# A trunk of split-precision projections: high weights taken over 576 columns as 320 and 256 instead of 288 twice

## The chip, the core and the metric

The kernel runs on one core of one Trainium2 chip. The metric is device time in microseconds for one execution. An execution ends when the last of the twelve outputs is in device memory. Five engines work side by side, each in the order of its own instructions, and wait for each other by semaphores: TensorE (PE in the profile, PEld for its weight loads), VectorE (DVE), ScalarE (ACT), GpSimd (POOL) and SyncE (SP), which here only issues DMAs.

## The reference, cut to what matters

The program is one inference step of a two-layer streaming encoder for two groups of requests with the same weights: 256 new frames of one stream ("prompt") and 32 next frames of another ("sample"). Everything is float32.

```
# layer 0: retention heads beside gated linear attention heads; layer 1: band attention
def trunk(x, ...):
    for l in range(2):
        h = rmsnorm(x, p['norm_mix_g'][l])
        mix = ab_mixer(h, ...) if l == 0 else c_mixer(h, ...)
        x = x + mix
        h = rmsnorm(x, p['norm_ffn_g'][l])
        f, buf = conv_ffn(h, ...)
        x = x + f
    return rmsnorm(x, p['norm_final_g']), ...

def conv_ffn(h, conv_buf, w_up, conv_w, conv_b, w_down):
    up = jnp.einsum('btd,df->btf', h, w_up)            # 2048 -> 2 x 5632
    g, u = jnp.split(up, 2, axis=-1)
    gp = jnp.concatenate([hist, g], axis=1)
    gc = conv_b
    for w in range(3):
        gc = gc + gp[:, w:w + T] * conv_w[w]
    act = jax.nn.silu(gc) * u
    return jnp.einsum('btf,fd->btd', act, w_down), ...  # 5632 -> 2048
```

Nearly all the arithmetic is in the projections: `w_in` (2048 to 7184), `w_out` twice (2048 to 2048), `w_qkv` (2048 to 6144), and for each layer `w_ffn_up` and `w_ffn_down`.

## The kernel before

Activations stand transposed: features on the 128 partitions, the 288 tokens (256 of the prompt, 32 of the sample, `T`) along the free dimension. A projection to 128 output features is one "product". It runs over its input features in k-tiles of 128 and accumulates in one PSUM bank, tile `acc`, of which there are four.

To keep more of float32's digits than the fast fp32r format holds, each operand is split in a high part, rounded to fp32r, and a low part, the rest. For each k-tile `passes` (L80 to L85) issues three fp32r matmuls of 288 columns: high weights on high activations (L83), high weights on low activations (L84), low weights on high activations (L85). In what follows these three are a triple. Two activation stores feed them: `x` tiles (normalized inputs, one tile for each k-tile, high part and low part side by side) and `b` tiles (mixer outputs and gated FFN activations, likewise).

`weights` (L54) loads a chunk of up to eight k-tiles of weights, 512 KB, by a DMA on SP's queue; ACT rounds it into `wh` (L61) and DVE subtracts to get `wl` (L62). There are four buffers of `w` and three each of `wh` and `wl`. `project` (L65) strings chunks together to a product, `input_product` calls it for the `x` tiles. Behind a product, DVE reads the sum out of PSUM: in `ffn` it scales it (L307, L308, L322) or adds it to the residual (L332), in `out_proj` it adds it to the residual (L284).

`first_products` (L87) starts the kernel: it brings input and first weights in ten DMAs whose borders are `cuts`, and computes three sums side by side, two ordinary products (L121, L123, L125) and one narrow one of two matmuls for each k-tile (L126, L127). Eight small matmuls of ones (L95) stand ahead of it.

The residual `x` is too large to stay in SBUF during the first mixer, so it is loaded a second time from `xT` ahead of the first `out_proj`: four DMAs of four k-tiles each (L220), on SP's queue and so in a row with the weights. `out_proj` finishes three products whose first half was computed earlier (`started`), adds each to `x`, and prepares the next norm (`norm_in`, and `norm_stat` at L193, whose matmul by ones sums the squares at the end of a layer's half).

The order of instructions on each engine is that of a scheduler that interleaves the program's lines by their dependences, so products of one head run while vector work of another is done.

Of the kernel before, what the change touches and what calls it, by code (L numbers as in the profile page):

```python
# [17 lines left out]
T = TP + TS  # L18
FF = 5632
NF = FF // P  # L20
HALF = NF // 2
# [5 lines left out]
N_FIRST = 2  # L27
WCH = 8
# [9 lines left out]
class Trunk:  # L38
# [15 lines left out]
    def weights(self, src, n, lo=False):  # L54
# [6 lines left out]
        nc.scalar.copy(h, w)  # L61
        nc.vector.tensor_tensor(l, w, h.bitcast(F32), op=ALU.subtract)  # L62
        return h, l

    def project(self, src, xh, xl, nk, k0=0, chunks=None, part=None, ps=None):  # L65

        if ps is None:
            ps = self.acc_ps.tile([P, 512], F32, name="acc", tag="acc")[:, :T]
        chunks = chunks or range(0, nk, WCH)
        for c in chunks if part is None else chunks[part : part + 1]:  # L70
            n = min(WCH, nk - c)
            h, l = self.weights(src[:, k0 + c : k0 + c + n, :], n)
            for j in range(n):
                first, last = c == chunks[0] and j == 0, c == chunks[-1] and j == n - 1
                self.passes(ps, h[:, j, :], l[:, j, :], xh[c + j], xl[c + j], first, last)
        return ps

    def input_product(self, w):
        return self.project(w, self.xh, self.xl, KD)

    def passes(self, ps, h, l, xh, xl, first, last):
        nc = self.nc
        nc.tensor.matmul(ps, lhsT=h, rhs=xh, start=first, stop=False)  # L83
        nc.tensor.matmul(ps, lhsT=h, rhs=xl, start=False, stop=False)  # L84
        nc.tensor.matmul(ps, lhsT=l, rhs=xh, start=False, stop=last)  # L85

    def first_products(self, src, xw, lo_h):  # L87


        nc = self.nc  # L90
        ps = [self.acc_ps.tile([P, 512], F32, name="acc", tag="acc")[:, :T] for _ in range(N_FIRST + 1)]
        cuts = (0, 1, 2, 3, 4, 6, 8, 10, 12, 14, 16)
# [3 lines left out]
        for c, (i, j) in enumerate(zip(cuts, cuts[1:])):  # L96
# [9 lines left out]
            for k in range(i, j):  # L106
# [13 lines left out]
                for o in range(N_FIRST):  # L120
                    nc.tensor.matmul(ps[o], lhsT=h[:, at, o, :], rhs=self.xh[k], start=first, stop=False)  # L121
                for o in range(N_FIRST):
                    nc.tensor.matmul(ps[o], lhsT=h[:, at, o, :], rhs=self.xl[k], start=False, stop=False)  # L123
                for o in range(N_FIRST):
                    nc.tensor.matmul(ps[o], lhsT=l[:, at, o, :], rhs=self.xh[k], start=False, stop=last)  # L125
                nc.tensor.matmul(ps[-1], lhsT=lo[:, at, :], rhs=self.xh[k], start=first, stop=False)  # L126
                nc.tensor.matmul(ps[-1], lhsT=lo[:, at, :], rhs=self.xl[k], start=False, stop=last)  # L127
        return ps
# [67 lines left out]
    def run(self, ctx):  # L196
# [4 lines left out]
        xs = [self.const(f"x{k}", [P, 2, T], F32R) for k in range(KD)]  # L201
        self.xh, self.xl = [[x[:, i, :] for x in xs] for i in range(2)]
        b_all = self.const("b", [P, KD, 2, T], F32R)
        self.bh_all, self.bl_all = b_all[:, :, 0, :], b_all[:, :, 1, :]
        self.bh, self.bl = [[b_all[:, k, i, :] for k in range(KD)] for i in range(2)]
# [9 lines left out]
        with self.tc.tile_pool(name="x", bufs=1) as xp:  # L215
# [3 lines left out]
            for k in range(0, KD, 4):  # L219
                nc.sync.dma_start(x[:, k : k + 4, :], a["xT"][:, k : k + 4, :])  # L220
            self.out_proj(a["w_out_ab"], 1, (WCH, 0))
# [24 lines left out]
    def out_start(self, w, chunks, n):  # L246

        self.started = [self.project(w[m], self.bh, self.bl, KD, chunks=chunks, part=0) for m in range(n)]

    def start(self, pool):  # L250
# [21 lines left out]
        v1 = self.mm()[:, :T]  # L272
        second = lambda part: self.project(w[VB + 1], self.xh, self.xl, KD, chunks=(0, WCH), part=part, ps=v1)
# [3 lines left out]
    def out_proj(self, w, n, chunks):  # L277

        for m in range(KD):
            if m < len(self.started):  # L280
                ps = self.project(w[m], self.bh, self.bl, KD, chunks=chunks, part=1, ps=self.started[m])
            else:
                ps = self.project(w[m], self.bh, self.bl, KD, chunks=chunks)
            self.nc.vector.tensor_tensor(self.x[m], self.x[m], ps, op=ALU.add)  # L284
            self.norm_in(m, n)
        self.norm_stat()

    def ffn(self, pool, layer, n, x_all):
        nc, a = self.nc, self.a
        bs = [self._one(pool, f"b{k}", [P, 2, T], None, F32R) for k in range(KD, HALF)]  # L290
        bh, bl = [old + [b[:, i, :] for b in bs] for i, old in ((0, self.bh), (1, self.bl))]
# [8 lines left out]
        for half in range(2):  # L300
            for fl in range(HALF):
# [23 lines left out]
                self.split(bh[fl], bl[fl], v)  # L325
# [4 lines left out]
            for m in range(KD):  # L330
                ps = self.project(down[m], bh, bl, HALF, half * HALF)
# [753 lines left out]
```

## Time and profile before

| | us |
|---|---|
| time, median of 3 runs | 2677.67 (2677.26 to 2677.90) |
| time of the profiled execution | 2679.3 |
| span of the profiled execution | 2677.2 |
| PE busy | 2661.0 |
| DVE busy | 1560.8 |
| ACT busy | 1126.1 |
| mean DMA rate | 167 GB/s |

The profile page gives for each group of instructions the line, engine, operation and tiles, the shape written, the count, then the total busy time and the mean duration of one, then the idle time of the engine just ahead of the group with what ended it. The timeline gives start, duration, engine, line and tiles of single instructions; a PE row's duration reaches to a modelled end, and matmuls overlap, so that the distance between two starts tells more than a duration. The view of stretches gives the length, then for each engine its busy time and, in brackets, how many instructions it ran, then the granted clock, the share of DMA time and GB/s.

### The profile page before, as it was taken

What the parts mean: (1) busy time and instruction counts of PE and PEld (TensorE: products, weight loads), DVE (VectorE), ACT (ScalarE), POOL (GpSimd) and SP (SyncE); (2) the same over time, 40 slices, a digit from 0 to 9 for tenths busy, and PEclk for the clock granted to TensorE, in tenths of its full rate; (3) what the DMA queues carried; (4) which work ended last, traced back from release to release, by engine and by line L of the source; (5) the groups of instructions that cost most, each with busy time, mean ns of one, the idle gap of its engine ahead of it and who ended that gap; (6) DMA issues with size and microseconds to landing.
All of it is one profiled execution on the core that took longest, in us unless ns stands there. A gap on an engine that the chain in (4) does not pass through costs nothing. (4 is left out here: it accounts for less than half of the span.)

```text
span 2677.2 us, 48712 instructions
## 1 busy us (share of the span) xinstructions
PE 2661.0 (99%) x20079; PEld 2642.5 (99%) x20079; DVE 1560.8 (58%) x2593; ACT 1126.1 (42%) x1511; POOL 132.8 (5%) x459
## 2 busy tenths in 40 slices
PE   9999999999999999999999999999999999999998
PEld 9999999999999999999999999999999999999998
DVE  8665555566664456665555555556666545666544
ACT  7564445443333333334444443444333333333443
POOL 3000000000000000000021110000000000000000
PEclk9999999999999999999999999999999999999999
DMA  6444445555555555555565565555555555555554
GB/s 230 151 138 156 157 157 193 167 164 166 166 166 164 167 168 167 165 168 160 166 213 179 178 183 166 158 166 165 166 166 166 163 167 168 166 166 166 165 166 131
DMA packets 127227, 448.27 MB, mean 167 GB/s; under 512 B 16059, under 2 KB 16379, under 8 KB 127004
## 3 DMA queue, kind: packets, MB, share of 16 engines
q1 hardware_dynamic: 119852, 426.83, 51.5%
q0 software_dynamic: 7008, 18.29, 2.2%
q8 instruction: 157, 2.57, 0.4%
q14 instruction: 66, 0.54, 0.1%
q10 hardware_dynamic: 144, 0.04, 0.0%
HBM read 434.69 MB, written 10.40 MB: 166 GB/s over the span
## 5 line engine op out<-in xcount | busy, mean ns | idle before, releaser
L61 ACT CAST wh<-w 128x1024 fp32r<-128x1024 f32 (+1 forms) x812 | 839.2, 1034 | 1461.0 <-PE acc L84 1210.8
L62 DVE TENSOR_TENSOR wl<-w,wh 128x1024 fp32r<-128x1024 f32 (+1 forms) x812 | 976.4, 1203 | 738.4 <-ACT wh L61 737.4
L83 PE MATMUL acc<-x,wh 128*128 128x288 f32 x4432 | 1314.6, 297 | 0.0
L84 PE MATMUL acc<-x,wh 128*128 128x288 f32 x4432 | 1311.8, 296 | 0.0
L85 PE MATMUL acc<-x,wl 128*128 128x288 f32 x4432 | 1308.4, 295 | 0.0
L85 PEld LDWEIGHTS acc<-x,wl 128*128 128x128 f32 x4432 | 839.5, 189 | 0.3
L83 PEld LDWEIGHTS acc<-x,wh 128*128 128x128 f32 x4432 | 833.0, 188 | 1.6 <-issue 1.1
L84 PEld LDWEIGHTS acc<-x,wh 128*128 128x128 f32 x4432 | 833.3, 188 | 0.3
L83 PE MATMUL acc<-b,wh 128*128 128x288 f32 x1920 | 567.4, 296 | 0.5 <-ACT wh L61 0.5
L85 PE MATMUL acc<-b,wl 128*128 128x288 f32 x1920 | 566.2, 295 | 0.7 <-DVE wl L62 0.7
L84 PE MATMUL acc<-b,wh 128*128 128x288 f32 x1920 | 566.9, 295 | 0.0
L85 PEld LDWEIGHTS acc<-b,wl 128*128 128x128 f32 x1920 | 363.2, 189 | 1.2 <-DVE wl L62 1.0
L83 PEld LDWEIGHTS acc<-b,wh 128*128 128x128 f32 x1920 | 360.6, 188 | 1.3 <-ACT wh L61 1.1
L84 PEld LDWEIGHTS acc<-b,wh 128*128 128x128 f32 x1920 | 360.8, 188 | 0.1
L316 DVE SCALAR_TENSOR_TENSOR gc<-gp,convp,gc 128x290 f32<-128x290 f32 x176 | 91.2, 518 | 3.1
L322 DVE TENSOR_TENSOR v<-acc,R 128x288 f32<-128x288 f32 x88 | 40.3, 458 | 88.6 <-PE acc L85 88.6
L307 DVE TENSOR_TENSOR gp<-acc,R 128x256 f32<-128x256 f32 x88 | 37.4, 425 | 90.3 <-PE acc L85 90.1
L309 POOL COPY conv_out<-gp 128x2 f32<-128x2 f32 x88 | 16.4, 187 | 1309.3 <-DVE gp L307 1309.3
L147 ACT CAST b<-v 128x288 fp32r<-128x288 f32 x88 | 38.2, 434 | 16.1 <-DVE v L324 16.1
L323 DVE TENSOR_TENSOR v<-v,sg 128x256 f32<-128x256 f32 x88 | 37.4, 426 | 10.6 <-DVE v L322 1.8
L314 DVE TENSOR_SCALAR gc<-gp,convp 128x290 f32<-128x290 f32 x88 | 38.0, 431 | 9.4
L332 DVE TENSOR_TENSOR x<-x,acc 128x288 f32<-128x288 f32 x64 | 29.1, 454 | 19.2 <-PE acc L85 19.2
(301 smaller groups left out, 1140.1 us busy)
## 6 DMA issues: line engine op xcount, KB each, us to landing
w<-in_w_ffn_up SPq DMA_DIRECT2D x352, 512.0 KB, 3.7
w<-in_w_ffn_down SPq DMA_DIRECT2D x128, 512.0 KB, 3.7
w<-in_w_in SPq DMA_DIRECT2D x108, 512.0 KB, 3.8
w<-in_w_qkv SPq DMA_DIRECT2D x96, 512.0 KB, 3.8
w<-in_w_ffn_down SPq DMA_DIRECT2D x64, 384.0 KB, 3.2
w<-in_w_out_ab SPq DMA_DIRECT2D x32, 512.0 KB, 3.9
w<-in_w_out_att SPq DMA_DIRECT2D x32, 512.0 KB, 3.7
xw<-in_x_first SPq DMA_DIRECT2D x6, 560.0 KB, 7.9
```

The costliest lines, as they stand in the source:

```text
L61: nc.scalar.copy(h, w)
L62: nc.vector.tensor_tensor(l, w, h.bitcast(F32), op=ALU.subtract)
L83: nc.tensor.matmul(ps, lhsT=h, rhs=xh, start=first, stop=False)
L84: nc.tensor.matmul(ps, lhsT=h, rhs=xl, start=False, stop=False)
L85: nc.tensor.matmul(ps, lhsT=l, rhs=xh, start=False, stop=last)
L147: self.nc.scalar.copy(h, v)
L307: nc.vector.tensor_tensor(gp[:, 2 : TP + 2], g[:, :TP], self.R[:, :TP], op=ALU.mult)
L314: nc.vector.tensor_scalar(gc, gp[:, 0:W], cw[:, 0:1], cw[:, 3:4], op0=ALU.mult, op1=ALU.add)
L316: nc.vector.scalar_tensor_tensor(gc, gp[:, w : w + W], cw[:, w : w + 1], gc, op0=ALU.mult, op1=ALU.add)
L322: nc.vector.tensor_tensor(v, u, self.R, op=ALU.mult)
L323: nc.vector.tensor_tensor(v[:, :TP], v[:, :TP], s[:, :TP], op=ALU.mult)
L332: nc.vector.tensor_tensor(self.x[m], self.x[m], ps, op=ALU.add)
```

## The change

High and low part of an activation tile become one row of 576 columns (`xx`, `bb`). `both` takes this row by the high weights in two matmuls: columns 0 to 319, and columns 320 to 575. The first 288 columns are the high part; so the first matmul also covers 32 columns of the low part and writes them into 32 extra columns of the PSUM bank (288 to 319), and the second writes the other 256 columns of the low part onto columns 32 to 287. `high` is the old third matmul, 288 columns by the low weights. When a product is complete, `joined` copies the 32 extra columns from PSUM to SBUF and adds them to columns 0 to 31, both on DVE.

The second load of the residual moves to POOL's queue. It comes in eight pieces of two k-tiles; two are issued at once, and the others one by one as products are finished: behind the residual add of product m, DVE copies one column of `x[m]` into the place of k-tiles 2m+4 and 2m+5, and the load of that piece has to wait for this copy. `cuts` has eight single k-tiles at the front instead of four.

```
+TX = 320
-    def passes(self, ps, h, l, xh, xl, first, last):
-        nc = self.nc
-        nc.tensor.matmul(ps, lhsT=h, rhs=xh, start=first, stop=False)
-        nc.tensor.matmul(ps, lhsT=h, rhs=xl, start=False, stop=False)
-        nc.tensor.matmul(ps, lhsT=l, rhs=xh, start=False, stop=last)
+    def both(self, ps, w, x, first, last=False):
+        nc = self.nc
+        nc.tensor.matmul(ps[:, :TX], lhsT=w, rhs=x[:, :TX], start=first, stop=last, skip_group_check=True)
+        nc.tensor.matmul(ps[:, TX - T : T], lhsT=w, rhs=x[:, TX:], start=False, stop=last, skip_group_check=True)
+
+    def high(self, ps, w, x, last):
+        self.nc.tensor.matmul(ps[:, :T], lhsT=w, rhs=x[:, :T], start=False, stop=last, skip_group_check=True)
+
+    def joined(self, ps):
+        n = TX - T
+        x = self.sp.tile([P, n], F32, name="tail", tag="tail", bufs=2)
+        self.nc.vector.tensor_copy(x, ps[:, T:TX])
+        self.nc.vector.tensor_tensor(ps[:, :n], ps[:, :n], x, op=ALU.add)
+        return ps[:, :T]
...
             for j in range(n):
                 first, last = c == chunks[0] and j == 0, c == chunks[-1] and j == n - 1
-                self.passes(ps, h[:, j, :], l[:, j, :], xh[c + j], xl[c + j], first, last)
-        return ps
+                self.both(ps, h[:, j, :], x[c + j], first)
+                self.high(ps, l[:, j, :], x[c + j], last)
+        return self.joined(ps) if part is None or part == len(chunks) - 1 else ps
...
-        cuts = (0, 1, 2, 3, 4, 6, 8, 10, 12, 14, 16)
+        cuts = (0, 1, 2, 3, 4, 5, 6, 7, 8, 10, 12, 14, 16)
...
                 for o in range(N_FIRST):
-                    nc.tensor.matmul(ps[o], lhsT=h[:, at, o, :], rhs=self.xh[k], start=first, stop=False)
+                    self.both(ps[o], h[:, at, o, :], self.xx[k], first)
                 for o in range(N_FIRST):
-                    nc.tensor.matmul(ps[o], lhsT=h[:, at, o, :], rhs=self.xl[k], start=False, stop=False)
-                for o in range(N_FIRST):
-                    nc.tensor.matmul(ps[o], lhsT=l[:, at, o, :], rhs=self.xh[k], start=False, stop=last)
-                nc.tensor.matmul(ps[-1], lhsT=lo[:, at, :], rhs=self.xh[k], start=first, stop=False)
-                nc.tensor.matmul(ps[-1], lhsT=lo[:, at, :], rhs=self.xl[k], start=False, stop=last)
-        return ps
+                    self.high(ps[o], l[:, at, o, :], self.xx[k], last)
+                self.both(ps[-1], lo[:, at, :], self.xx[k], first, last)
+        return [self.joined(p) for p in ps]
...
-            for k in range(0, KD, 4):
-                nc.sync.dma_start(x[:, k : k + 4, :], a["xT"][:, k : k + 4, :])
-            self.out_proj(a["w_out_ab"], 1, (WCH, 0))
+            self.out_proj(a["w_out_ab"], 1, (WCH, 0), x)
...
-    def out_proj(self, w, n, chunks):
+    def out_proj(self, w, n, chunks, load=None):
+        nc = self.nc
+        def piece(k, n):
+            nc.gpsimd.dma_start(load[:, k : k + n, :], self.a["xT"][:, k : k + n, :])
+        if load is not None:
+            piece(0, 2)
+            piece(2, 2)
         for m in range(KD):
...
-            self.nc.vector.tensor_tensor(self.x[m], self.x[m], ps, op=ALU.add)
+            nc.vector.tensor_tensor(self.x[m], self.x[m], ps, op=ALU.add)
+            k = 2 * m + 4
+            if load is not None and k < KD:
+                nc.vector.tensor_copy(load[:, k : k + 2, :1], load[:, m : m + 1, :1].to_broadcast([P, 2, 1]))
+                piece(k, 2)
             self.norm_in(m, n)
```

On PE, in a down-projection of a ConvFFN, these rows stand before the change (line, operation, tiles written and read, shape written):

```order
L83 MATMUL acc<-b,wh 128x288
L84 MATMUL acc<-b,wh 128x288
L85 MATMUL acc<-b,wl 128x288
L83 MATMUL acc<-b,wh 128x288
L84 MATMUL acc<-b,wh 128x288
L85 MATMUL acc<-b,wl 128x288
```

and these after it:

```order
L91 MATMUL acc<-b_6410,wh 128x320
L92 MATMUL acc<-b_6410,wh 128x256
L95 MATMUL acc<-b_6410,wl 128x288
L91 MATMUL acc<-b_6411,wh 128x320
L92 MATMUL acc<-b_6411,wh 128x256
L95 MATMUL acc<-b_6411,wl 128x288
```

The order and the count of the matmuls are the same; the widths of the first two differ, and a triple still covers 864 columns.

On DVE, in the down-projection, these rows stand before (`wl` is the low part of the weights, the third row the residual add):

```order
L62 TENSOR_TENSOR wl<-w,wh 128x768
L62 TENSOR_TENSOR wl<-w,wh 128x1024 x2
L332 TENSOR_TENSOR x<-x,acc 128x288
L62 TENSOR_TENSOR wl<-w,wh 128x768
L62 TENSOR_TENSOR wl<-w,wh 128x1024 x2
L332 TENSOR_TENSOR x<-x,acc 128x288
```

and these after:

```order
L63 TENSOR_TENSOR wl<-w,wh 128x768
L63 TENSOR_TENSOR wl<-w,wh 128x1024 x2
L100 COPY tail<-acc 128x32
L101 TENSOR_TENSOR acc<-acc,tail 128x32
L356 TENSOR_TENSOR x<-x,acc 128x288
L63 TENSOR_TENSOR wl<-w,wh 128x768
```

Copy and add of the 32 columns stand between the last low weights of the next product and the residual add that reads the sum; it is now the copy that waits for PE.

On SP, around the second load of the residual, these rows stand before:

```order
L60 DMA w<-in_w_in 128x1024 x108
L60 DMA w<-in_w_out_ab 128x1024 x10
L220 DMA x<-in_xT 128x1152 x4
L60 DMA w<-in_w_out_ab 128x1024 x22
L60 DMA w<-in_w_ffn_up 128x1024 x88
```

and these on POOL after the change (the rows of `gp` and `hist` belong to the ConvFFN that follows):

```order
L294 DMA x<-in_xT 128x576 x2
L548 DMA convp<-in_convp 128x176
L548 DMA hist<-in_hist 128x88
L321 MEMSET gp_6420 128x2
L321 MEMSET gp_6421 128x2
L321 MEMSET gp_6422 128x2
L330 COPY gp_6420<-hist 128x2
L330 COPY gp_6421<-hist 128x2
L330 COPY gp_6422<-hist 128x2
L294 DMA x<-in_xT 128x576 x6
```

The four loads no longer stand between weights on SP. Two pieces come first on POOL, six behind the ConvFFN's small preparations.

More of the change, by code (lines that the diff above doesn't have):

```diff
@@ L52, in const, with weights @@
         return t
-    def weights(self, src, n, lo=False):
+    def weights(self, src, n):
         nc = self.nc
@@ L63, in weights, with project @@
         return h, l
-    def project(self, src, xh, xl, nk, k0=0, chunks=None, part=None, ps=None):
+    def project(self, src, x, nk, k0=0, chunks=None, part=None, ps=None):
         if ps is None:
-            ps = self.acc_ps.tile([P, 512], F32, name="acc", tag="acc")[:, :T]
+            ps = self.acc()
         chunks = chunks or range(0, nk, WCH)
@@ L200, in run @@
         self.ones, self.eps = ones[:, :P], ones[:, P : P + 1]
[L201 to L205, printed above, removed]
+        self.xx = [self.const(f"x{k}", [P, 2 * T], F32R) for k in range(KD)]
+        self.xh, self.xl = [[x[:, c] for x in self.xx] for c in (slice(0, T), slice(T, 2 * T))]
+        b_all = self.const("b", [P, KD, 2 * T], F32R)
+        self.bh_all, self.bl_all = b_all[:, :, :T], b_all[:, :, T:]
+        self.bb, self.bh, self.bl = [[x[:, k, :] for k in range(KD)] for x in (b_all, self.bh_all, self.bl_all)]
         self.R = self.const("R", [P, T])
@@ L246, in out_start @@
     def out_start(self, w, chunks, n):
-        self.started = [self.project(w[m], self.bh, self.bl, KD, chunks=chunks, part=0) for m in range(n)]
+        self.started = [self.project(w[m], self.bb, KD, chunks=chunks, part=0) for m in range(n)]
     def start(self, pool):
@@ L289, in ffn @@
         nc, a = self.nc, self.a
-        bs = [self._one(pool, f"b{k}", [P, 2, T], None, F32R) for k in range(KD, HALF)]
-        bh, bl = [old + [b[:, i, :] for b in bs] for i, old in ((0, self.bh), (1, self.bl))]
+        bb = self.bb + [self._one(pool, f"b{k}", [P, 2 * T], None, F32R) for k in range(KD, HALF)]
         convp = self._one(pool, "convp", [P, NF, 4], a["convp"][:, layer])
```

18 lines of the change are left out of this document (10 added, 8 removed).

## The prediction

> **What bounds the kernel now.** I read the page's busy shares first, then its groups, then the stretch of layer 0's ConvFFN with each engine's instructions counted.
>
> ```profile
> span 2677.2 us, 48712 instructions
> PE 2661.0 (99%) x20079; PEld 2642.5 (99%) x20079; DVE 1560.8 (58%) x2593; ACT 1126.1 (42%) x1511; POOL 132.8 (5%) x459
> L61 ACT CAST wh<-w 128x1024 fp32r<-128x1024 f32 (+1 forms) x812 | 839.2, 1034 | 1461.0 <-PE acc L84 1210.8
> L62 DVE TENSOR_TENSOR wl<-w,wh 128x1024 fp32r<-128x1024 f32 (+1 forms) x812 | 976.4, 1203 | 738.4 <-ACT wh L61 737.4
> L83 PE MATMUL acc<-x,wh 128*128 128x288 f32 x4432 | 1314.6, 297 | 0.0
> L84 PE MATMUL acc<-x,wh 128*128 128x288 f32 x4432 | 1311.8, 296 | 0.0
> L83 PE MATMUL acc<-b,wh 128*128 128x288 f32 x1920 | 567.4, 296 | 0.5 <-ACT wh L61 0.5
> ...
> 540.00:1376.00 836.00, 836.00 (x6307) 836.00 (x6307) 485.51 (x730) 325.01 (x390) 22.27 (x131) 1.00 0.55 166
> ```
>
> TensorE (PE) is busy all the time, and its matmuls follow with no idle time before them. The 297 ns of one matmul is no cost, because matmuls overlap; the pitch is. In the last row 6307 matmuls start in 836 us, so one starts every **132.6 ns**. ScalarE (ACT) waits 1210.8 us for PE to hand back weight buffers and VectorE (DVE) waits 737.4 us for ACT, so both run ahead of PE and are held by it. Only a shorter pitch shortens the kernel by much.
>
> **What a matmul of 288 columns costs, and why.** Three kinds of rows tell: the cold start, f32 matmuls (two steps of the array a column in each record), and a weight load after a wait.
>
> ```profile
> 3.99 0.85 PE L95 MATMUL mm<-ones 128*128 128x128 f32 x3
> L95 PE MATMUL mm<-ones x16: 421/421/582, 1.1 to 4.4; 128*128 128x128 f32 x16
> 4.89 0.44 PE L121 MATMUL acc<-x,wh 128*128 128x288 f32 x1
> 5.13 0.48 PE L123 MATMUL acc<-x,wh 128*128 128x288 f32 x1
> 5.20 0.32 PEld L123 LDWEIGHTS acc<-x,wh 128*128 128x128 f32 x1
> 5.44 0.31 PE L123 MATMUL acc<-x,wh 128*128 128x288 f32 x1
> 1472.34 0.27 PE L880 MATMUL mm<-ident,as 128*128 128x128 f32 x1
> 1472.45 0.27 PE L881 MATMUL mm<-ident,as 128*128 128x128 f32 x1
> 1472.56 0.27 PE L882 MATMUL mm<-ident,as 128*128 128x128 f32 x1
> 1457.20 0.59 PE L889 MATMUL mm<-ap,avt 128*128 128x256 f32 x2
> 1457.63 0.38 PE L890 MATMUL mm<-ap,avt 128*128 128x128 f32 x2
> 2663.50 0.65 PE L193 MATMUL mm<-ssq,ones 128*128 128x288 f32 x2
> L193 PE MATMUL mm<-ssq,ones x2: 405/406/406, 2663.5 to 2663.7; 128*128 128x288 f32 x2
> 6.87 0.19 PEld L123 LDWEIGHTS acc<-x,wh 128*128 128x128 f32 x1
> 6.98 0.30 PE L123 MATMUL acc<-x,wh 128*128 128x288 f32 x1
> ```
>
> At full rate f32 records of 128 columns follow at 0.11 us, of 256 at (1457.63 - 1457.20)/2 = 0.215, of 288 at 0.65 - 0.406 = 0.244. So 32 columns more cost about 27 ns: 64 steps, 0.417 ns a step, and about 2 ns fixed for each record. At the start L95's 128 columns take (0.85 - 0.421)/2 = 0.214: the array ran at half rate. There a 288-column fp32r matmul takes 0.24 us (4.89 to 5.13; weights at 5.20, next start at 5.44), which is 288 steps of 0.833 ns and nothing over.
>
> At full rate 288 steps are 120 ns and 2 ns fixed make 122; the trace has 132.6. The surplus of 10.6 ns is not a number of array cycles for each matmul (at half rate it would show as 20 ns), and f32 at 288 columns hasn't got it. It isn't the weights either: after a wait a matmul starts 0.11 us after its load began (6.87, 6.98). Two readings are left:
>
> - **Remainder.** The array takes columns in blocks, and a block does not go in less than 132.6 - 256 x 0.417 = 25.9 ns. In 288 columns the last 32 are such a short block (13.3 ns of work). At half rate those 32 take 26.7 ns, in f32 too: no surplus, as the rows show. 320 and 256 columns have no short block if blocks are of 64.
> - **Rate.** The operand arrives no faster than 132.6/288 = 0.46 ns a column whatever the array's clock; that too is hidden at half rate and in f32.
>
> ```profile
> 560.00:800.00 240.00, 240.00 (x1813) 240.00 (x1812) 150.53 (x246) 94.21 (x113) 9.40 (x57) 1.00 0.53 165
> 830.00:920.00 90.00, 90.00 (x681) 90.00 (x681) 39.87 (x41) 30.41 (x31) 0.00 (x0) 1.00 0.60 167
> ```
>
> With DVE busy 63% and 44% of a stretch, and DMA 0.53 and 0.60, the pitch stays within 0.2% (132.4 and 132.2, counting edges). A supply from a memory that all share should vary with its other users, so I choose the remainder; nothing here excludes the rate.
>
> The Trainium skill (TensorE: Matmul & The Clock Gate, Back-to-back issue gap) gives a warm gap of N/2.4 + 2.5 ns: 122.5 ns here. The trace's 132.6 disagrees; by that rule nothing is gained, since columns and matmuls are as many after as before, and the time would be the one of the rate rival below. The Trainium skill (TensorEngine Tiling (Array Packing), Instruction Overhead) says that a matmul of one column takes as long as one of 60; were the last 32 columns charged so, an estimate from it is 106.7 + 25 = 131.7 ns, near the row, but no run here shows that it holds inside a matmul.
>
> **The change part by part.**
>
> *Matmuls.* How many triples (high weights on high, high weights on low, low weights on high):
>
> ```profile
> L83 PE MATMUL mm<-x,wh 128*128 128x288 f32 x16 | 4.9, 308 | 0.0
> L121 PE MATMUL acc<-x,wh 128*128 128x288 f32 x32 | 7.7, 319 | 0.5 <-ACT wh L110 0.5
> L126 PE MATMUL acc<-x,lo_h 128*128 128x288 f32 x16 | 4.6, 295 | 0.0
> ```
>
> 4432 + 1920 + 16 + 32 = 6400 triples, and 16 pairs without the third. Before, the first two cost 265.2 ns. After, 320 columns: 133.3 + 2 = 135.5. 256 columns: 106.7 + 2, but each has its own weight load, and rows at 1472 repeat load and matmul at 110: I take 110. Together 245.5, so 19.7 ns saved, times 6416 = **126 us**. Bounds of this case: 133.3 + 106.7 saves 25.2 (161 us); 138 + 112, a slower load and an unknown 3 ns at 320, saves 15.2 (97 us). The 288-column third matmul stays at 132.6. No matmul or weight load is added.
>
> *Join.* Each of 376 products gets a DVE copy of 32 columns and an add of 32.
>
> ```profile
> L308 DVE TENSOR_TENSOR gp<-acc,R 128x32 f32<-128x32 f32 x88 | 15.9, 180 | 0.0
> 2664.68 0.75 PE L193 MATMUL mm<-sql,ones 128*128 128x288 f32 x2 [0.54 <-ACT sql L179]
> ```
>
> 2 x 0.18 = 0.36 us each, 135 us of DVE in all. What hides it is DVE's 738 us of waiting; with it DVE is at 1696 of some 2550 us. Queued behind the copy, which waits for PE's last matmul, are the consumers and the next low weights; these are ahead by the buffers above. Exposed it is where PE itself waits for a product's consumer: at the four sums of squares that close a layer, like the last (L193, 2664.68). 4 x 0.36 = +1.5 us. Without cover it would be 135 us.
>
> *Reload of the residual.*
>
> ```profile
> 448.38 1.85 SPq L220 DMA_DIRECT2D x<-in_xT  x4
> 452.80 0.82 DVE L284 TENSOR_TENSOR x<-x,acc 128x288 f32<-128x288 f32 x2 [3.84 <-DMA x<-in_xT]
> 456.00 0.29 PE L85 MATMUL acc<-b,wl 128*128 128x288 f32 x1
> 456.80 0.40 PE L83 MATMUL acc<-b,wh 128*128 128x288 f32 x1 [0.50 <-ACT wh L61]
> 457.04 0.29 PE L84 MATMUL acc<-b,wh 128*128 128x288 f32 x1
> 458.06 0.40 PE L85 MATMUL acc<-b,wl 128*128 128x288 f32 x1 [0.73 <-DVE wl L62]
> 458.30 0.29 PE L83 MATMUL acc<-b,wh 128*128 128x288 f32 x1
> ```
>
> DVE waits 3.84 us for x, weights queue behind it, and four matmuls take 2.30 us where 0.53 would do: 1.77 us lost. After, GpSimd (POOL) issues the pieces, a quarter of x first, and SP's weights no longer stand behind them. I take -1.8 us; the other end is +1.8, if POOL's pieces come later than SP's did. Later pieces are asked for 4 products ahead, some 24 us, and the six 2-column copies of DVE are under the join's price.
>
> *Cuts of the start.* Four more single k-tiles, two more DMAs on SP.
>
> ```profile
> 8.00:9.00 1.00, 0.71 (x5) 0.45 (x4) 0.40 (x2) 0.85 (x2) 0.21 (x1) 1.00 0.99 403
> 9.00:10.00 1.00, 0.75 (x5) 0.59 (x5) 1.00 (x3) 1.00 (x3) 0.33 (x2) 1.00 1.00 403
> ```
>
> PE is idle 0.54 us here, but DMA is full (403 GB/s): nothing taken, between -0.5 and +0.5.
>
> *Supply.* A chunk of 512 KB serves 24 matmuls: 3.18 us now, 3.02 then. DMA goes from 166 to some 174 GB/s, of the 403 above. ACT's 1.03 and DVE's 1.20 us a chunk fit.
>
> **Sum:** -126 + 1.5 - 1.8 = -126.3. The profiled execution took 2679.3 us by its own time (span 2677.2), 1.6 over the median of 2677.67 shown. 2679.3 - 126.3 = 2553, less those 1.6 = **2551 us**.
>
> **The rivals.**
>
> - *Only 256 columns lose the surplus* (a limit at 256, not at each 64): 320 cost 133.3 + 12.6 = 146, so 9.2 ns a triple, 59 us: **2618**. Nothing in the trace has over 288 columns, so nothing speaks against it.
> - *Rate: the change doesn't do what its split is for.* 864 columns at 0.46 ns before and after; -0.3 us of the rest: **2677**. For it: cold and f32 rows fit. Against it: the constant pitch.
> - *Slower: weights become the floor.* If a load next to a running matmul holds the next start back to 132.6 ns, the 256-column matmul costs 132.6 still and the 320-column one 135.5: +2.9 x 6416 = +19: **2696**. It decides once the array's work is under the load's hold. For it: loads and matmuls alternate one to one (x6307 each). Against it: 0.11 us at 6.87, and the f32 rows at 0.11 with a load each.
>
> **How the numbers follow.** Remainder 0.62, limit at 256 0.13, rate 0.14, weights 0.11. The forecast is the likeliest, 2551, by itself 2516 to 2580. The range has to reach the rate case to leave out less than 2 in 10: 2520 to 2680. About 0.2% (5.4 us) is what a measurement can tell from no change: faster 0.75, same 0.14, slower 0.11.
>
> **What would show it.** The pitch after L91 (320 columns) should be 134 to 138 ns, after L92 (256) 107 to 112, after L95 132.6; the rate gives 147, 118 and 132.6, the weights' floor 135, 132.6 and 132.6. The copy at L100 should wait for PE, with PE never waiting for DVE outside the layer ends; at the reload the four matmuls should take 0.6 us. I am wrong if L92's pitch is over 118.

## The result, and the profile after

| | before | after |
|---|---|---|
| time, median (lowest to highest), us | 2677.78 (2677.26 to 2679.14), 4 runs | 2656.47 (2656.01 to 2659.25), 4 runs |
| ratio to before, 95% interval | | 0.9922 (0.9905 to 0.9939) |
| time of the profiled execution, us | 2679.3 | 2656.71 |
| DVE busy, us | 1560.8 | 1708.6 |

21 us less, 0.8%: faster, as forecast, but only a sixth of the 126 us. The page of the changed kernel, busy shares and groups:

```profile
span 2654.9 us, 49383 instructions
PE 2636.5 (99%) x20079; PEld 2618.0 (99%) x20079; DVE 1708.6 (64%) x3355; ACT 1123.6 (42%) x1511; POOL 228.9 (9%) x471
...
L91 PE MATMUL acc<-x,wh 128*128 128x320 f32 x4464 | 1394.9, 313 | 0.3 <-DVE x L185 0.3
L62 ACT CAST wh<-w 128x1024 fp32r<-128x1024 f32 (+1 forms) x812 | 838.8, 1033 | 1288.1 <-PE acc L92 1044.7
...
L100 DVE COPY tail<-acc 128x32 f32<-128x32 f32 x376 | 72.0, 192 | 285.7 <-PE acc L95 282.9
...
L101 DVE TENSOR_TENSOR acc<-acc,tail 128x32 f32<-128x32 f32 x376 | 74.8, 199 | 12.1
```

PE is still the bound (99%), with as many matmuls as before. ACT still waits for PE, and the join (L100, L101) costs DVE 147 us that lie beside PE: L100 waits for PE's last matmul, and PE's groups have next to no idle time. So the pitch is what counts again. First the stretches of the ConvFFN (length, PE busy and matmuls, granted clock, DMA), then the timeline of single matmuls (start, duration, line):

```profile
560.00:800.00 240.00, 240.00 (x1833) 1.00 0.54 167
830.00:920.00 90.00, 90.00 (x689) 1.00 0.58 166
```

```profile
453.05 0.28 PE L92 MATMUL acc<-b,wh 128*128 128x256 f32 x1
453.16 0.29 PE L95 MATMUL acc<-b,wl 128*128 128x288 f32 x1
453.29 0.31 PE L91 MATMUL acc<-b,wh 128*128 128x320 f32 x1
453.44 0.28 PE L92 MATMUL acc<-b,wh 128*128 128x256 f32 x1
453.56 0.29 PE L95 MATMUL acc<-b,wl 128*128 128x288 f32 x1
455.75 0.55 PE L91 MATMUL acc<-b,wh 128*128 128x320 f32 x1 [1.90 <-ACT wh L62]
456.09 0.42 PE L92 MATMUL acc<-b,wh 128*128 128x256 f32 x1
457.00 0.61 PE L95 MATMUL acc<-b,wl 128*128 128x288 f32 x1 [0.50 <-DVE wl L63]
457.41 0.47 PE L91 MATMUL acc<-b,wh 128*128 128x320 f32 x1
```

1833 matmuls start in 240 us where 1813 did. The first rows show one triple as it runs where nothing waits: 0.15 us behind the 320 columns, 0.12 behind the 256, 0.13 behind the 288 (149, 116 and 128 ns, from all starts in the trace). The first two take 265 ns, as two of 288 did. The only matmul that became cheaper is the one that wasn't changed. Over all triples without a wait (under 440 ns from start to start of L91; before of L83) the mean went from 397.64 to 393.39 ns: 4.25 ns times 6400 is 27 us, more than the whole gain. The rest of this document is about those 4 ns.

The other rows are the reload: four matmuls from 453.56 to 457.41 take 3.85 us where 0.52 would do. 3.3 us are lost, where the kernel before lost 1.77. DVE and POOL there:

```profile
452.52 0.82 DVE L304 TENSOR_TENSOR x<-x,acc 128x288 f32<-128x288 f32 x2 [5.89 <-DMA hist<-in_hist]
```

```profile
446.79 1.08 POOL L294 DMA_DIRECT2D x<-in_xT  x2 [4.51 <-DMA out_ret_out<-rst]
...
455.23 0.43 POOL L330 COPY gp<-hist 128x2 f32<-128x2 f32 x3 [6.13 <-DMA hist<-in_hist]
455.60 1.07 POOL L294 DMA_DIRECT2D x<-in_xT  x2
```

POOL issues the first pieces after waiting 4.51 us for the stores of the retention state to land, and the residual add that reads them starts 5.73 us after their issue; DVE has waited 5.89 us. (The row puts the wait down to `hist`, the load behind them on the same queue; the add reads only `x` and PSUM.) Two more pieces stand behind a copy on POOL that waits 6.13 us for that load; PE shows no loss from these. The wait for the stores isn't new. Before the change SP's reload had it too (view of SP's waits: total, times, longest):

```profile
SPq L220 <- DMA out_ret_out<-rst: 6.4, 3, 5.3
```

From the landing of the last store to the issue of the reload, the traces have 0.2 us on SP before and 0.8 us on POOL after.

### The profile page after: what moved, and what is told of

Its sections match the earlier page's. It is cut to its first block, busy times and chain, and to the rows that moved or that the text cites. A ratio compares the mean times of both kernels' runs of the same rounds, so it can differ in the third digit from the quotient of the medians.

```text
span 2654.9 us, 49383 instructions
## 1 busy us (share of the span) xinstructions
PE 2636.5 (99%) x20079; PEld 2618.0 (99%) x20079; DVE 1708.6 (64%) x3355; ACT 1123.6 (42%) x1511; POOL 228.9 (9%) x471
## 4 chain that ended last, share of the span: by engine, by line
PE 87%; issue 11%; DMA 0%; DVE 0%; POOL 0%; ACT 0%; DVEq 0%; POOLq 0%; ACTq 0%
PE acc L91 32%; PE acc L95 28%; PE acc L92 25%; PE mm L599 0%; PE mm L913 0%; PE mm L877 0%; DMA x<-in_xT 0%; DMA out_ret_out<-rst 0%; DVE y L370 0%; PE mm L876 0%; PE mm L207 0%; PE mm L914 0%; DMA gains<-in_gains 0%; PE mm L91 0%; PE mm L513 0%
## 5 line engine op out<-in xcount | busy, mean ns | idle before, releaser
L91 PE MATMUL acc<-x,wh 128*128 128x320 f32 x4464 | 1394.9, 313 | 0.3 <-DVE x L185 0.3
L92 PE MATMUL acc<-x,wh 128*128 128x256 f32 x4464 | 1246.5, 279 | 0.0
L91 PEld LDWEIGHTS acc<-x,wh 128*128 128x128 f32 x4464 | 838.4, 188 | 2.3 <-issue 1.1
L92 PEld LDWEIGHTS acc<-x,wh 128*128 128x128 f32 x4464 | 838.5, 188 | 0.8 <-issue 0.3
L91 PE MATMUL acc<-b,wh 128*128 128x320 f32 x1920 | 599.0, 312 | 1.9 <-ACT wh L62 1.9
L92 PE MATMUL acc<-b,wh 128*128 128x256 f32 x1920 | 536.6, 280 | 0.0
L91 PEld LDWEIGHTS acc<-b,wh 128*128 128x128 f32 x1920 | 361.6, 188 | 2.7 <-ACT wh L62 2.4
L92 PEld LDWEIGHTS acc<-b,wh 128*128 128x128 f32 x1920 | 361.6, 188 | 0.0
L100 DVE COPY tail<-acc 128x32 f32<-128x32 f32 x376 | 72.0, 192 | 285.7 <-PE acc L95 282.9
L333 POOL COPY conv_out<-gp 128x2 f32<-128x2 f32 x88 | 100.3, 1140 | 1272.5 <-DVE gp L331 1272.5
L101 DVE TENSOR_TENSOR acc<-acc,tail 128x32 f32<-128x32 f32 x376 | 74.8, 199 | 12.1
L162 DVE TENSOR_TENSOR b<-v,b 128x288 fp32r<-128x288 f32 x88 | 40.5, 460 | 44.0 <-ACT b L161 44.0
```

Of the source, the lines that this page charges most:

```text
L91: nc.tensor.matmul(ps[:, :TX], lhsT=w, rhs=x[:, :TX], start=first, stop=last, skip_group_check=True)
L92: nc.tensor.matmul(ps[:, TX - T : T], lhsT=w, rhs=x[:, TX:], start=False, stop=last, skip_group_check=True)
L100: self.nc.vector.tensor_copy(x, ps[:, T:TX])
L101: self.nc.vector.tensor_tensor(ps[:, :n], ps[:, :n], x, op=ALU.add)
L162: self.nc.vector.tensor_tensor(l, v, h.bitcast(F32), op=ALU.subtract)
L333: nc.gpsimd.tensor_copy(conv_out[:, f, 0:2], gp[:, TP : TP + 2])
```

## The experiments

**Bursts behind the end.** To read a pitch where nothing else runs, the changed kernel got matmuls of its own behind its last store: 48 at a time, each time with four narrow ones as a mark. `one` is a matmul of n columns, from operand column `at` to PSUM column `to`.

```
+        for n in (512, 448, 384, 352, 320, 304, 296, 288, 280, 272, 264, 256, 248, 240, 224, 192, 160, 128, 64):
+            mark()
+            for k in range(48):
+                one(ps, h[:, k % WCH, :], k, n, 0, 0)
...
+        for t in triples:
+            mark()
+            for k in range(16):
+                for (n, at, to), w in zip(t, (h, h, l)):
+                    one(ps, w[:, k % WCH, :], k, n, at, to)
```

> The changed kernel with bursts of 48 matmuls of one width behind its end, from 512 to 64 columns, at other operand columns and other PSUM columns, then 16 triples each of several splits; PE has nothing to wait for there. Pitch of a burst = its first start to the first start behind it, over 48. The remainder theory of the prediction: 288 at 132.6 ns, 320 at 135.5, 256 at 108 to 110, a step of the pitch at each 64 columns. The rate theory: 0.46 ns a column at every width (512 at 235, 320 at 147, 256 at 118, 128 at 59). A rate with a fixed part: a straight line with an intercept of some ns. If the 4 ns that the low weights' matmul lost in the changed kernel come from the operand's address, the burst of 288 at operand column 288 differs from that at column 0 or 256; if from where the matmul before it writes in PSUM, the burst that alternates two banks, or the triple in two banks, is shorter than 132.6 and 397.6; if from a long matmul ahead, the triples 352/224, 384/192, 448/128, 512/64 go on falling below 393.4.

Start to start, the mean over the last 36 of 48 matmuls, worked out from the trace:

```
columns   512   448   384   352   320   304   296   288   280   272   264   256   248   240   224  192  160  128
ns      233.3 202.2 174.7 160.0 146.6 138.6 140.0 133.3 128.3 123.3 120.0 117.8 120.0 113.3 111.7 111.7 111.7 111.7
triples: 288/288/288 397.8   320/256/288 393.3   256/320/288 399.2   352/224/288 406.7   512/64/288 473.3
```

No step at 64 columns, and 288 is not dear: 320 costs 146.6, 256 costs 117.8, together 264.4 against 266.7. The memory is idle here, so no other user of it makes the rate, 0.455 ns a column at 512 and 352 columns. Below 240 columns a floor of 111.7 ns shows whatever the width; I take it for the weight load, one for each matmul. But the values aren't a line either: 296 columns cost more than 304, and 248 as much as 264. All triples are near whole multiples of 6.67 ns or of a third of it (59 x 6.67 = 393.3, 60 x 6.67 = 400). And 320/256/288 reproduces the kernel's 393.39, 288/288/288 its 397.64.

**The parts of the change alone.** `e2_even` is the changed kernel with TX = 288 and no join. `e3_widths_only` takes back reload and cuts. `e5_reload` takes back the reload alone.

```
e2_even:        -TX = 320
                +TX = 288
                ... (joined returns at once when no column is left over)
e3, e5:         +            for k in range(0, KD, 4):
                +                nc.sync.dma_start(x[:, k : k + 4, :], a["xT"][:, k : k + 4, :])
                -            self.out_proj(a["w_out_ab"], 1, (WCH, 0), x)
                +            self.out_proj(a["w_out_ab"], 1, (WCH, 0))
e3 as well:     -        cuts = (0, 1, 2, 3, 4, 5, 6, 7, 8, 10, 12, 14, 16)
                +        cuts = (0, 1, 2, 3, 4, 6, 8, 10, 12, 14, 16)
```

> The changed kernel with TX = 288: 288 and 288 columns again, no join, reload and cuts as changed. If the widths bring the whole gain, the time is that of the kernel before plus the 4 us that PE lost at the reload and the start: 2680 to 2683 us, a triple at 397.6 ns. If the gain sits in the reload, the cuts or the order of the operand's halves: 2655 to 2660, a triple near 393.

> The changed kernel with the residual's reload on SP in four pieces and the start's cuts as before; widths and join stay. If the reload in pieces costs the 4 us that its stalls show: 2651 to 2654 us. If the stalls there are shifted from elsewhere and the reload costs nothing: 2656 to 2657. If the reload gains the 1.8 us of the prediction: 2658 to 2659.

> The changed kernel with the reload on SP as before; widths, join and the finer cuts stay. If the reload in pieces costs 3.9 us by itself, as its stalls say: 2652 to 2653, like the kernel with widths alone. If the cuts cost a part of that: 2653.5 to 2656.

| | median (lowest to highest), us | ratio to before |
|---|---|---|
| e2_even | 2679.39 (2677.22 to 2680.55), 11 runs | 1.0009 (1.0001 to 1.0018) |
| the change | 2656.47 (2656.01 to 2659.25) | 0.9922 (0.9905 to 0.9939) |
| e5_reload | 2654.16 (2653.11 to 2655.28), 5 runs | 0.9917 (0.9903 to 0.9930) |
| e3_widths_only | 2652.54 (2652.31 to 2652.83), 4 runs | 0.9909 (0.9894 to 0.9924) |

The whole gain comes with the two widths; reload and cuts give some of it back. The intervals overlap, since the kernel before itself scatters from 2674.5 to 2680.7, but the times of the last three are apart by more than their own scatter: 2.3 us for the reload, 1.6 for the cuts. (`e3_widths_only` and `e5_reload` ran on different chips, but all three traces have the same triple, 393.4 ns.) The first is what PE loses in the trace. `e2_even` misses its 2680 to 2683 narrowly. With the reload on SP (`e3_widths_only`, timelines of SP, DVE and PE):

```profile
445.96 1.82 SPq L234 DMA_DIRECT2D x<-in_xT  x4
```

```profile
450.25 0.82 DVE L306 TENSOR_TENSOR x<-x,acc 128x288 f32<-128x288 f32 x2 [3.72 <-DMA x<-in_xT]
```

```profile
453.74 0.28 PE L92 MATMUL acc<-b,wh 128*128 128x256 f32 x1
454.75 0.40 PE L95 MATMUL acc<-b,wl 128*128 128x288 f32 x1 [0.72 <-DVE wl L63]
454.98 0.31 PE L91 MATMUL acc<-b,wh 128*128 128x320 f32 x1
```

The add starts 4.3 us after the issue and not 5.73, and PE loses 1.0 us there (1.24 for two steps that take 0.24) instead of 3.3. So POOL's reload is issued 0.6 us later behind the stores and used 1.4 us later behind its issue, though its first piece is half as large: 2.0 of the 2.3 us.

The cuts' place is the first sum of squares (L207), which waits for DVE. In the changed kernel, in `e3_widths_only`, and in `e2_even`, which has the finer cuts but no join:

```profile
28.34 0.29 PE L95 MATMUL acc<-x,wl 128*128 128x288 f32 x1
30.54 0.72 PE L207 MATMUL mm<-xw,ones 128*128 128x288 f32 x2 [1.91 <-issue]
```

```profile
29.41 0.29 PE L95 MATMUL acc<-x,wl 128*128 128x288 f32 x1
30.39 0.72 PE L207 MATMUL mm<-xw,ones 128*128 128x288 f32 x2 [0.69 <-PE acc L95]
```

```profile
28.42 0.29 PE L95 MATMUL acc<-x,wl 128*128 128x288 f32 x1
28.56 0.65 PE L209 MATMUL mm<-xw,ones 128*128 128x288 f32 x2
```

With finer cuts PE is through its first products earlier (28.34 against 29.41), but the sum of squares isn't ready any earlier: 2.20 us between the starts against 0.98. `e5_reload` keeps the cuts, and its trace has 2.21 there. The last rows show that the cuts alone don't do this: without the join the sum is ready at 28.56, and PE waits for nothing. With it, DVE comes to the last addition ahead of the sum of squares 2.3 us later (at 29.98 against 27.72), without idle time; which part of its work moved isn't followed further.

**Order, address, type.** If the 4 ns are the pattern of a sequence, swapping the two matmuls must cost time. A second set of bursts moved operands and PSUM columns, and took bf16 operands. The swap in the kernel:

```
-        nc.tensor.matmul(ps[:, :TX], lhsT=w, rhs=x[:, :TX], start=first, stop=last, skip_group_check=True)
-        nc.tensor.matmul(ps[:, TX - T : T], lhsT=w, rhs=x[:, TX:], start=False, stop=last, skip_group_check=True)
+        parts = ((x[:, :TX], ps[:, :TX]), (x[:, TX:], ps[:, TX - T : T]))
+        for i, (xs, to) in enumerate(parts if first else parts[::-1]):
+            nc.tensor.matmul(to, lhsT=w, rhs=xs, start=first and i == 0, stop=last, skip_group_check=True)
```

> The changed kernel with the 256 columns ahead of the 320 (but in the first k-tile of a product). The remainder theory: no difference, 2656 us. If the gain of 4.2 ns is the rounding of a sequence: 399.2 instead of 393.3 ns a triple, 6400 x 5.8 ns = +37 us: 2692 to 2695, slower than the kernel before.

> Again the changed kernel with bursts behind its end: 16 triples each (high, high, low weights) of many widths, operand columns and PSUM columns, then 48 matmuls each of bf16 operands. In the first run of bursts a column cost 0.455 ns (512 columns 233.3, 352 160.0) and each matmul beyond that 0 to 7 ns (288 133.3, 296 140.0, 264 120.0), the means near whole thirds of 20 ns: a beat of 6.67 ns to which a sequence rounds up. The beat theory expects triples of 864 columns at 392.7 ns and up, in steps of a few ns that depend on order and width (288/288/288 397.8, 320/256/288 393.3, 256/320/288 399.2 again), and no saving with 304/272 that grows with anything but the rounding. If the operand's address decides, the triples of 288 with the second operand at column 256 or 272 fall to 393. If the PSUM column decides, those written from column 32 do. bf16: if the 0.455 ns are the fetch of 4-byte operands, 512 bf16 columns take 214 to 216 ns (0.417 a column); if it is the array or PSUM, 233.

`e4_swapped`: 2692.32 us (2691.05 to 2693.34), ratio 1.0059 (1.0045 to 1.0073). The same two matmuls in the other order make the kernel slower than the one before, and 36 us slower than the change; the bursts' 5.9 ns a triple come to 38. The stretch from 500 to 1350 us shows it for PE, before, after and swapped:

```profile
500.00:1350.00 850.00, 849.84 (x6409) 1.00 0.55 166
```

```profile
500.00:1350.00 850.00, 850.00 (x6481) 1.00 0.56 167
```

```profile
500.00:1350.00 850.00, 850.00 (x6387) 1.00 0.53 165
```

Three times 850 us by the count is the triple: 397.9, 393.5, 399.2 ns. The second set of bursts, in ns:

```
288/288/288, second operand at column 288: 397.8; 256: 400.0; 272: 395.6; 280: 400.0; 284: 396.7
            written from PSUM column 8, 16, 32, 64, 128: 397.8 each
            first and third at column 16: 393.3; 32: 395.0; 64: 397.8
304/272/288 397.8   312/264/288 395.7   296/280/288 399.4   328/248/288 400.2   336/240/288 396.7
bf16 columns  512   448   384   320   304   288   256   224   192   160
ns          215.8 189.2 162.5 135.8 129.2 122.5 109.2  95.8  82.5  69.2
```

PSUM columns change nothing; the operand's column does, and a move by 64 columns (256 bytes) is none. My guess that 256 or 272 would be the good columns was wrong. In bf16 a column costs 0.417 ns and a matmul 2.5 ns, at each width to 0.1 ns, with no pattern: so 0.455 and the patterns come with the 4-byte operands. The bf16 bursts changed the moving operand and the weights together. That the moving operand's column changes the pattern speaks for the moving one; weights at other addresses were not tried. Nor is less always faster: 320/256/280 took 396.7 ns, more than 320/256/288.

The Trainium skill (TensorE: Matmul & The Clock Gate, Back-to-back issue gap) gives N/2.4 + 2.5 ns as the gap of an isolated warm matmul; in bf16 the bursts agree, each matmul with its own weight load (215.8 for 512), in fp32r they do not (233.3). For a stream of loads and matmuls the same section of the Trainium skill has 131 ns at 512 columns, which no burst here shows.

**The address as a knob.** All operand tiles are moved on inside their lines (a line is 64 columns, 256 bytes, the move that changed nothing): first in bursts, then in the kernel BEFORE, with its own widths (`e7_shift20`, `e7_shift44`).

```
-        xs = [self.const(f"x{k}", [P, 2, T], F32R) for k in range(KD)]
-        b_all = self.const("b", [P, KD, 2, T], F32R)
+        xb = self.const("xb", [P, 2 * KD * 2 * T + 64], F32R)[:, SHIFT : SHIFT + 2 * KD * 2 * T]
+        xb = xb.rearrange("p (s k i t) -> p s k i t", s=2, k=KD, i=2)
+        x_all, b_all = xb[:, 0], xb[:, 1]
... (the further b tiles of the ConvFFN likewise)
```

> Bursts behind the changed kernel's end again: 16 triples of 288/288/288 columns with both operands moved on by i = 0, 4, ... 60 columns (the low one at 224 + i, which is 288 + i less 64, since a move of the high one by 64 changed nothing: 397.8), then high at i and low at 224 + j for 0, 16, 32, 48, then 320/256/288 moved on by 0, 8, ... 56, then bursts of one width (288, 256) at columns 0, 16, 32, 48. If the time is columns x 0.4545 ns and a rounding that the operand's address within 64 columns (256 bytes) sets: 0/224 repeats the 397.8 of 0/288, 16/224 the 393.3 of 16/288, the others lie from 392.7 to 400, and some shift of both operands, with the widths of the kernel before, comes to 394 or less. If the address within a 64-column line has nothing to do with it and the ranges' overlap made the 393.3: all shifts by i give 397.8. For 320/256/288 the first theory expects other values than 393.3 at some shifts.

> The kernel BEFORE (288 columns thrice, reload and cuts as before), with all operand tiles x and b moved on by 20 columns (80 bytes) within their 256-byte lines; weights, residual and the rest keep their places within a line. If the address sets the rounding, as in the bursts (393.3 ns at a shift of 20 against 397.8 at 0): 6400 x 4.5 ns less, 2647 to 2650 us, with no new width and no join. If the bursts' order of weights or their start made it: 2677.

> The same with 44 columns (176 bytes). By the bursts a triple takes 406.7 ns there: 6400 x 8.9 ns more, 2732 to 2736 us. If the address has nothing to do with it: 2677.

The bursts gave 288/288/288 at 393.3 ns for a shift of 20, 406.7 for 44, and values in between for the others. The kernels did not follow, neither the 2647 to 2650 forecast at 20 nor the 2732 to 2736 at 44: 2668.93 us at 20 (2655.05 to 2670.35, six runs; 0.9962, 0.9948 to 0.9977), and at 44 ten runs from 2639.5 to 2713.0, all with a granted clock of 0.998 or 0.999. (The ratio for the latter, 0.9928, 0.9897 to 0.9959, leaves out the two longest, so it says little; the other eight still go from 2639.5 to 2678.2.) No other kernel here scatters like this. The profiled executions, 2655.05 and 2712.97, at 20 and at 44:

```profile
500.00:1350.00 850.00, 849.82 (x6480) 1.00 0.55 168
```

```profile
500.00:1350.00 850.00, 849.78 (x6278) 1.00 0.53 162
```

393.5 and 406.2 ns: in this stretch these two sat in the patterns of the bursts. The other executions have no trace; I took it that they sat in others. So the next bursts entered each sequence behind eight different lead-ins.

> Bursts behind the changed kernel's end: eight sequences of 16 triples, each eight times behind a single matmul of another width (130 to 512 columns), so each is entered in eight phases. If a sequence's time is set by widths and addresses alone: eight equal values for each (397.8 for 288/288/288, 393.3 for it at a shift of 20, 406.7 at 44, 396.7 at 60, 393.3 for 320/256/288, 399.2 for 256/320/288). If the phase in which a sequence is entered picks one of several patterns: values of one sequence differ, 393.3 beside 400.

```
shift  triple       behind a lead-in of 130, 200, 250, 300, 330, 400, 470, 512 columns
 0     288/288/288  397.8 397.8 397.8 396.7 397.8 397.8 397.8 396.7
20     288/288/288  393.3 400.0 393.3 393.3 393.3 393.3 393.3 400.0
44     288/288/288  406.7 390.0 390.0 390.0 390.0 390.0 406.7 390.0
60     288/288/288  396.7 in all
 0     320/256/288  393.3 in all
 0     256/320/288  400.0 in all
```

Entered differently, the same instructions fall into one pattern or another and stay there. At shift 44 the two are 16.7 ns apart, 107 us over 6400 triples, room enough for one kernel to take 2639.5 or 2713. The trace of the 2712.97 us has both ends: 392 ns a triple from 200 to 300 us, in the mixer, and 406.7 in both ConvFFNs. The kernel before has a small choice (396.7 or 397.8, 7 us over 6400 triples, about as much as it scatters). `e2_even`, the same widths, shows that choice within one execution, by the ConvFFN of layer 0 and of layer 1:

```profile
600.00:1300.00 700.00, 700.00 (x5282) 1.00 0.54 165
1900.00:2600.00 700.00, 700.00 (x5296) 1.00 0.54 166
```

From all starts that is 397.8 and 396.7 ns a triple, each kept throughout. The change's sequence showed one pattern behind every lead-in. That it has no other isn't shown: with the second operand one line earlier it took 393.3 behind the same eight lead-ins, but 400.0 in `p3_phase`.

> Bursts behind the changed kernel's end: 14 triples each of n / 576 - n / 288 columns, for n = 288 and 320 at operand shifts of 0, 4, ... 60 columns behind six lead-in matmuls each, for n = 304, 312, 336 at shifts of 0, 8, ... 56 behind four. If a sequence locks to a pattern and the lead-in picks among several (as 390.0 or 406.7 at a shift of 44): values per sequence that lie on few steps (390.0, 393.3, 396.7, 400, 406.7), some sequences with one value whatever the lead-in, 320/256 at shift 0 among them at 393.3, and 288/288 at shift 0 at 396.7 or 397.8. A sequence with one value below 393.3 would make a faster kernel than the changed one: 6400 x 3.3 = 21 us for 390.0. If the patterns are only a matter of the end of this kernel (no other load on the memory): no prediction from them holds in a whole kernel, which the run after this tests.

The mean of the last six of the 14 triples, lowest and highest over the lead-ins:

```
shift            0     4     8    12    16    20    24    28    32    36    40    44    48    52    56    60
288/288 lowest  396.7 393.3 396.7 393.3 395.3 393.3 400.0 396.7 400.0 393.3 400.0 390.0 396.7 400.0 395.5 396.2
       highest  397.8 400.0 400.0 396.7 398.0 400.0 400.0 400.0 400.0 400.0 400.0 406.7 396.7 400.0 395.7 397.0
320/256 lowest  393.3 396.7 400.0 400.0 395.5 393.3 396.7 394.8 393.3 396.7 397.7 403.3 393.3 391.5 393.3 400.0
       highest  393.3 400.0 400.0 400.0 395.7 393.3 400.0 397.2 400.0 396.7 400.0 403.3 400.0 394.2 393.3 400.0
```

Over all 16 shifts and six lead-ins the mean is 397.9 ns for the old widths and 396.9 for the new: the widths as such are worth some 1 ns, and by the spread over the shifts (a standard error of 0.8) it may be nothing. The kernel before happens to sit at an average place, the changed one at a good place for its widths. No sequence tried, those of 304, 312 and 336 columns among them, stayed below 393.3 behind every lead-in (320/256 at 52 wavers between 391.5 and 394.2).

Two whole kernels at shifts where the map has a single value settle it: the kernel before at 56, and the change's widths (as `e3_widths_only`) at 44. For the latter a whole line of padding doesn't fit into SBUF (`e8_wide44`, which gave no time); `e8b_wide44` pads less and comes to the same column of a line.

> The kernel BEFORE with its operand tiles 56 columns on, where the bursts of 288/288/288 have one pattern, 395.5 ns, whatever the lead-in: 6400 x 2.3 ns less than 397.8, 2660 to 2663 us, close together, unlike those at 20 and 44, which had two patterns each in the bursts and 15 and 70 us of scatter in the kernel. If the address decides nothing: 2677.

> The kernel with the widths alone (320 and 256, join; reload and cuts as before the change) and all operand tiles 44 columns on within their lines; in the bursts 320/256/288 has one pattern there, 403.3 ns, whatever the lead-in. If the address decides in the whole kernel too: 2652.5 + 6400 x 10.0 ns = 2714 to 2718 us in every run, slower than the kernel before with the very widths of the change. If 320 and 256 columns are cheaper as such: 2652.

```profile
500.00:1350.00 850.00, 849.84 (x6444) 1.00 0.54 166
```

```profile
500.00:1350.00 850.00, 850.00 (x6329) 1.00 0.52 164
```

`e9_shift56`: 2667.28 us (2666.99 to 2667.60), 0.9965 (0.9951 to 0.9979), 395.7 ns a triple. `e8b_wide44`: 2707.84 us (2706.99 to 2709.96), 1.0115 (1.0098 to 1.0132), 402.9 ns. Both are as close together as the map lets one expect, on their sides of the kernel before, with triples as in the bursts; the times miss the expectations by 4 and 6 us. (At 44 the mixers fall below 403.3 in places, 398 to 402 ns over stretches of 100 us, the ConvFFN does not.) So 320 and 256 columns make this kernel 0.9% faster at one address and 1.2% slower at another.

The fastest steady kernel is `e3_widths_only`, 2652.5 us: the widths with the old reload and cuts, 24 us under the kernel before and 4 under the change.

## Why the prediction was wrong

- **The bound** was right: PE's pitch, with DVE and ACT ahead of it. What the widths gained is all pitch, 27 us.
- **The step that failed** is "I choose the remainder", and with it the term of 19.7 ns a triple. It measured 4.25. L92's pitch is 116 ns, under the 118 at which I had called myself wrong, but L91's is 149 and not 134 to 138. Bursts show no block of 64 columns; the rival "rate" has the first two matmuls right (265 ns), and the second table of bursts bears it out: fp32r operands come at 0.455 ns a column, bf16 at 0.417. The half rate of the start I had read from the pitch alone, for the granted clock shows 1.00 there; `p1_widths` has it with a granted clock of 0.50, and 288 fp32r columns follow there at 240 ns, 0.833 a column and nothing over, as a limit of the supply would have it.
- **Why I chose it**: the pitch stayed within 0.2% in stretches of unlike DVE and DMA load, and I took that against a supply limit. The bursts have the same rate with no load at all: the limit doesn't come from other users of the memory. The inference from "constant" to "not the supply" was wrong.
- **What the rate rival missed** are the patterns. It gives 2677; the 4.25 ns come from the widths, order and address of the three operands together, which neither reading knew of. My forecast had the sign right for a reason that doesn't exist.
- **Weights as the floor**: there is one, 111.7 ns in fp32r; I had taken 110 from rows of f32. At 256 columns it doesn't bind.
- **Join**: cover held, 147 us of DVE beside PE. Of the four ends only the last shows it. Between the first matmul of L207 and its last wait lay 1.18 us before; after:

```profile
2641.10 0.65 PE L207 MATMUL mm<-ssq,ones 128*128 128x288 f32 x2
...
2642.74 0.51 PE L207 MATMUL mm<-sql,ones 128*128 128x288 f32 x1 [0.99 <-ACT sql L193]
```

  1.64, so +0.46. At the other three PE has the next products' matmuls to run. The start has a fifth place, which I had not named: 0.98 us ahead of L207 in `e3_widths_only` and 2.20 in the change, where the kernel before has 0.13.
- **Reload**: -1.8 forecast, its other end +1.8 given; PE lost 3.3 us there instead of 1.77, so +1.6 against the kernel before, and +2.3 against the change without it. What failed is the step from a smaller first load to an earlier one. POOL waits for the stores of `rst` as SP did, issues 0.6 us later behind them, and has 1.4 us more from issue to use.
- **Cuts**: 0 within 0.5 forecast; about +1.6 with the join behind them. PE gets its products earlier, and waits the longer for DVE. Without the join (`e2_even`) there is no such wait.
- **Sum**, against the kernel before: -27.2 for the pitch, +1.6 reload, +2.1 at the start (join and cuts) and +0.5 last end make -23.0. The spans of the two profiled executions are 22.3 us apart, the medians 21.3; the kernel before alone scatters by 6.

## What to carry to other kernels

Where a kernel is bound by back-to-back fp32r matmuls, count 0.455 ns a column (0.44 to 0.48 in bursts of one width from 240 columns up) and take what a sequence of widths, orders and addresses makes of it from bursts, entered in several ways; then lay the operands where there is only one pattern and it is a good one. A gain of a per cent from other matmul widths may be a gain of address: move the operands by some columns before believing in the widths. And when a load moves to another queue, look first at how long it takes there from what releases it to its use: here 2 us more on POOL's queue than on SP's.

## What was not expected of the hardware

- One stream of fp32r matmuls can have several stable patterns, and in the traces keeps the one it fell into through a whole ConvFFN: 390.0 or 406.7 ns a triple in bursts, 2639.5 to 2713.0 us for the kernel. Most are whole multiples of 3.33 ns (390.0, 393.3, 396.7, 400.0, 403.3, 406.7), some are not (395.0, 397.8). What beats against what there wasn't found; PSUM columns, banks (397.8 with two) and other engines, idle in the bursts, are not it.
- The clock fell in the burst of 64 columns, once, in the one run that has it. Stretches inside that burst, and across its end into the next of 288 columns:

```profile
2783.00:2787.00 4.00, 4.00 (x38) 1.00 0.00 0
2788.00:2793.00 5.00, 5.00 (x23) 0.50 0.00 0
```

  PE was never idle, but 64 columns are some 27 ns of work (an estimate, 64 x the 0.417 of bf16) in a pitch of 112. After 41 such matmuls the granted clock went to 0.50, and then 288 columns started at 240 ns for 16 matmuls. That the little work for each matmul did it isn't shown.
